# The last triangular system on GpSimd, the third with a shorter lag, and W_down's sums from the second head pair on

## The chip, the core and the metric

The kernel runs on one core of a Trainium2 chip. A core has five engines that each work off a queue of their own in order: TensorE (PE), VectorE (DVE), ScalarE (ACT), GpSimd (POOL), and SyncE (SP), which here only starts DMAs. The metric is the device time of one execution in microseconds; lower is better.

## The reference

One layer of a trunk with two parallel branches, over 1024 tokens of width 1024, in float32. Cut to what matters:

```python
h = rmsnorm(x, g_mix[i]);  z = h @ w_in[i]
q, k, v = ...                                   # 8 FoX heads of 64, q and k RMS-normed
log_f = jax.nn.log_sigmoid(zf[..., 3 * FOX_WIDTH:] + b_f[i])
y_fox = fox_attention(q, k, v, log_f)           # causal, bias c_i - c_j, c = cumsum(log_f)
yr = rwkv7_scan(rh, decay, kh, vh, -kk, kk * ah)    # 8 heads, state 64 x 64, step by step
merged = gate_fox * (y_fox @ w_o_fox[i]) + gate_rwkv * (y_rwkv @ w_o_rwkv[i])
x = x + merged @ w_out[i]
x = x + (gelu(u[..., :D_FF]) * u[..., D_FF:]) @ w_down[i]      # u: conv of rmsnorm(x) @ w_up
x = x + sigmoid(rmsnorm(x) @ w_ple_gate) * (p @ w_ple_up)
```

## The kernel before

The RWKV scan is done in chunks of 64 tokens. For each of four head pairs `rwkv_pre` projects r, k and v and builds, per chunk and head, a lower triangular system that is stored to HBM as `Ad`. `tsolve` inverts its two 32 x 32 diagonal blocks for all 16 chunks and both heads of a pair at once: it loads them as `tA` (four DMAs), copies the start into `tT` on GpSimd, and then makes 30 steps that depend on each other, each a product into `tt` and a sum into `tT`. Step j has ((j+1)//2) x (31-j) elements in each partition, 15 to 128, 2600 over all steps. The result goes to HBM as `Td`, and, turned by two ScalarE copies into `tX`, as `Ud`. The systems of head pairs 0 to 2 run beside `rwkv_pre` of the next pair, the last one beside attention's first projections.

Attention works in head pairs too. `fox_z` projects q, k and v (and, for pair 0, the forget inputs `ft`) in eight blocks of 128 tokens, called block 0 to 7 here. Each block takes one PSUM tile z of a pool of two. ScalarE copies it out (z, V, ft, sq) and VectorE takes V's rest and sums (ss); after blocks 3 and 7 sm, a square root (st) and a few small VectorE operations give the scale, and GpSimd scales four blocks of z at once (L759). `gate_early` makes 512 columns of a gate in one z tile, so its two halves take the tiles of blocks 6 and 7. `forget` turns ft into the forget row: ScalarE's abs, exp and ln (fe), L908 and L909 on VectorE, the prefix fpre, two products on PE (L917, L918), a copy fc, two transposes (L927) and a store (`cd`), which comes back as cb, spread over all partitions; VectorE adds it to the scores. `fox_qk` turns z into q and k, and is interleaved with `forget` and the gate. `fox_w` of the next pair splits weights in two parts (fwh, fwl), the second of three on GpSimd.

`down_sums` prepares W_down for a product scheme with fewer multiplications: for each of 11 pairs of blocks it loads two rows of blocks into `wt`, makes four subtractions on GpSimd and stores four sums as `wd`. It has one buffer.

Which work is emitted beside which is set by `interleave`, in which each part names its costs and a total, and the part that is least far along comes next:

```python
    live = [[g, n, 0.0] for g, n in parts]
    while live:
        it = min(live, key=lambda e: e[2] / e[1])
        try:
            it[2] += next(it[0]) or 0.0
```

A lag such as `yield self.tlag` is a cost without work. Emission isn't the last word: the framework that builds the program places instructions in each engine's queue by estimates of its own, so that the first six pairs of `down_sums` stand in GpSimd's queue under the RWKV part, where no code names them. The functions that the diff touches:

Of the kernel before, what the change touches and what calls it, by code (L numbers as in the profile page):

```python
# [20 lines left out]
P = 128  # L21
# [6 lines left out]
HP = 4  # L28
DFF = 2816
NFB = DFF // P  # L30
# [22 lines left out]
def flat(gens):  # L53
    for g in gens:
        yield from g
# [7 lines left out]
def interleave(*parts):  # L63
# [7 lines that stand above are left out]
        except StopIteration:  # L71
            live.remove(it)


def merge(*gens):

    live = list(gens)
    while live:
        for g in list(live):
            try:  # L80
                yield next(g)
            except StopIteration:
                live.remove(g)


class Net:
# [409 lines left out]
    def tsolve(self, hp):  # L496

        nc, tp = self.nc, self.tp
        tA = tp.tile([P, 32, 32], F32, name="tA", tag="tA", bufs=1)
        tT = tp.tile([P, 16, 32], F32, name="tT", tag="tT", bufs=1)
        tX = tp.tile([P, 32, 16], F32, name="tX", tag="tX", bufs=1)
        tmp = tp.tile([P, 144], F32, name="tt", tag="tt", bufs=1)
        Ad, Td, Ud = self.Ad[hp], self.Td[hp], self.Ud[hp]
        for q in range(2):
            for d in range(2):  # L510
                p0 = q * 64 + d * 32
                ds = slice(d * 32, d * 32 + 32)
                nc.sync.dma_start(tA[p0:p0 + 32], Ad[ds, :, ds].rearrange("s b t -> b s t"))
        yield self.tlag
        for q in range(2):
            r = slice(q * 64, q * 64 + 64)
            nc.gpsimd.tensor_copy(tT[r], tA[r, q:32:2, :])
        for j in range(1, 31):
            n, m = 31 - j, (j + 1) // 2
            tv = tmp[:, 0:m * n].rearrange("p (c i) -> p c i", i=n)  # L520
            nc.vector.tensor_mul(tv, tA[:, j:j + 1, j + 1:32].broadcast_to([P, m, n]),
                                 tT[:, 0:m, j:j + 1].broadcast_to([P, m, n]))
            nc.vector.tensor_add(tT[:, 0:m, j + 1:32], tT[:, 0:m, j + 1:32], tv)
            yield (2 * m * n / 960.0 + 0.13)
        for q in range(2):
            r = slice(q * 64, q * 64 + 64)
            nc.vector.memset(tT[r].rearrange("p a b -> p (a b)")[:, q:512:34], 1.0)
            for d in range(2):
                nc.sync.dma_start(Td[d, :, q:32:2, :], tT[q * 64 + d * 32:q * 64 + d * 32 + 32])
            r = slice(q * 64, q * 64 + 32)  # L530
            nc.scalar.copy(tX[r].rearrange("p b m -> p m b"), tT[r])
            nc.sync.dma_start(Ud[:, :, q * 16:q * 16 + 16], tX[r])
# [903 lines left out]
    def body(self, stop):  # L1436
        nc, a = self.nc, self.a
# [63 lines left out]
        self.cw = 160.0  # L1501
        self.lora_w()
        self.p1, close_p1 = self.pool("rw", side="right")
        self.tlag = 30.0
        for hp in range(HP):
            side = [(self.tsolve(hp - 1), 40.0)] if hp else []
            if hp == HP - 1:
# [9 lines left out]
        self.fp, close_fp = self.pool("fox", side="right")  # L1517
        self.kl = None
        zV, qk = [], []
        self.tlag = 12.0  # L1520
        self.wt, close_wt = self.pool("wt", side="left")
        self.wd2 = {n: self.tc.dram_tile([NFB // 2, P, 512], F32, name="wd" + n) for n in ("t1", "t2", "t3", "t4")}

# [3 lines left out]
        for hp in range(HP):  # L1527
            att = self.fox_att(hp, qk, zV[1])
            if hp + 1 < HP:
                zV, qk = [], []  # L1530
                interleave((att, 23.0), (self.fox_z(hp + 1, self.fox_w(hp + 1), zV), 31.5),
                           (self.down_sums(range(hp * 4, min(hp * 4 + 4, NFB // 2))), 12.0),
                           *([(flat([self.tmerge(2 * hp - 2, z_tile), self.tmerge(2 * hp - 1, z_tile)]), 24.0)] if hp else []))
                interleave((merge(self.last, flat([[0.0] * 3, self.fox_qk(zV[0], qk)])), 6.0), (self.gate_early(hp + 2), 10.4))
            else:
                n = HP + 1

                def rest():
                    yield from att
                    yield from self.last  # L1540
                interleave((rest(), 25.0), (flat([self.gate_early(j) for j in range(n, self.early)]),
                                            10.4 * (self.early - n)))
        close_ps()
        close_fp()
        close_fwp()
# [68 lines left out]
        m = []  # L1614
# [150 lines left out]
        for q in range(2):  # L1765
            for tb in range(4):
                if q == 0:
                    b = next(hi)
# [44 lines left out]
```

## Time and profile before

| | us |
|---|---|
| runs, median of 3 | 1881.25 (1880.01 to 1883.6) |
| profiled execution, its own time | 1872.82 |
| its span, first to last instruction | 1870.9 |
| PE busy | 1807.9 |
| VectorE busy | 1205.0 |
| ScalarE busy | 782.7 |
| GpSimd busy | 356.4 |

Of a row of a timeline the first number is the start, the second the duration, both in us; in brackets stands how long the engine was idle before it, and what it waited for. Durations and gaps belong to the profiled execution, the medians to separate runs without a profile. Names are those of the tiles, with L and a line number of the kernel before. After the change lines behind the first edit are two higher.

### The profile page before, as it was taken

What the parts mean: (1) busy time and instruction counts of PE and PEld (TensorE: products, weight loads), DVE (VectorE), ACT (ScalarE), POOL (GpSimd) and SP (SyncE); (2) the same over time, 40 slices, a digit from 0 to 9 for tenths busy, and PEclk for the clock granted to TensorE, in tenths of its full rate; (3) what the DMA queues carried; (4) which work ended last, traced back from release to release, by engine and by line L of the source; (5) the groups of instructions that cost most, each with busy time, mean ns of one, the idle gap of its engine ahead of it and who ended that gap; (6) DMA issues with size and microseconds to landing.
All of it is one profiled execution on the core that took longest, in us unless ns stands there. A gap on an engine that the chain in (4) does not pass through costs nothing.

```text
span 1870.9 us, 28292 instructions
## 1 busy us (share of the span) xinstructions
PE 1807.9 (97%) x10867; PEld 1484.4 (79%) x10867; DVE 1205.0 (64%) x2382; ACT 782.7 (42%) x1236; POOL 356.4 (19%) x251
## 2 busy tenths in 40 slices
PE   6999998799999999999999999999999999999999
PEld 5877778688988776666778988888888888888898
DVE  7537754767565734544436188999899986566752
ACT  4543252567676631122362244434343344434431
POOL 4321001330000000000013303554444531000000
PEclk9999999899999999999999999999999999999999
DMA  6667447542221255444375123333223328755431
GB/s 199 204 190 200 130 108 197 151 157 81 46 75 48 60 142 150 131 137 132 95 258 169 62 91 85 113 109 101 91 96 116 102 96 315 238 194 178 145 114 46
DMA packets 295085, 250.29 MB, mean 134 GB/s; under 512 B 80200, under 2 KB 235550, under 8 KB 294951
## 3 DMA queue, kind: packets, MB, share of 16 engines
q1 hardware_dynamic: 230071, 220.40, 37.4%
q10 hardware_dynamic: 64880, 28.09, 5.9%
q8 instruction: 86, 1.41, 0.3%
q14 instruction: 48, 0.39, 0.1%
HBM read 171.07 MB, written 77.37 MB: 133 GB/s over the span
## 4 chain that ended last, share of the span: by engine, by line
PE 65%; DVE 2%; DMA 2%; ACT 1%; issue 1%; SPq 0%; POOL 0%; ACTq 0%; DVEq 0%; POOLq 0%
PE pu L1155 8%; PE pu L1156 8%; PE pu L1157 8%; PE pu L1333 3%; PE pu L1332 3%; PE pu L1331 3%; PE zt L228 3%; PE zt L229 3%; PE zt L227 3%; PE zt L986 2%; PE zt L988 2%; PE zt L236 2%; PE zt L237 2%; PE zt L987 2%; PE zt L238 2%; PE yps L636 1%
## 5 line engine op out<-in xcount | busy, mean ns | idle before, releaser
L1331 PE MATMUL pu<-op 128*128 128x512 f32 x276 | 107.7, 390 | 0.0
L1333 PE MATMUL pu<-op 128*128 128x512 f32 x276 | 107.4, 389 | 0.0
L1332 PE MATMUL pu<-op 128*128 128x512 f32 x276 | 107.4, 389 | 0.0
L207 ACT CAST wh<-wr 128x1024 fp32r<-128x1024 f32 (+1 forms) x43 | 38.1, 890 | 123.2 <-PE zt L237 78.0
L236 PE MATMUL zt<-hah,wh 128*128 128x512 f32 (+1 forms) x200 | 80.6, 404 | 0.0
L237 PE MATMUL zt<-hal,wh 128*128 128x512 f32 (+1 forms) x200 | 78.8, 394 | 0.0
L236 PE MATMUL zt<-hbh,wh 128*128 128x512 f32 (+1 forms) x200 | 78.8, 394 | 0.0
L237 PE MATMUL zt<-hbl,wh 128*128 128x512 f32 (+1 forms) x200 | 78.3, 391 | 0.0
L238 PE MATMUL zt<-hbh,wl 128*128 128x512 f32 (+1 forms) x200 | 78.1, 390 | 0.0
L238 PE MATMUL zt<-hah,wl 128*128 128x512 f32 (+1 forms) x200 | 77.7, 389 | 0.0
L1165 DVE SCALAR_TENSOR_TENSOR u<-c,par,u 128x1023 f32<-128x1023 f32 x44 | 73.5, 1672 | 3.4 <-ACT u L1164 3.4
L208 DVE TENSOR_TENSOR op<-vh,op 128x1024 fp32r<-128x1024 f32 x38 | 45.4, 1222 | 45.1 <-ACT op L207 31.7
L1164 ACT ACTIVATE u<-c,par 128x1024 f32<-128x1024 f32 x44 | 54.6, 1243 | 47.5 <-DVE c L1241 37.6
L1166 DVE SCALAR_TENSOR_TENSOR u<-c,par,u 128x1022 f32<-128x1022 f32 x44 | 73.5, 1672 | 0.7
L1155 PE MATMUL pu<-hah,wh 128*128 128x512 f32 x176 | 70.3, 400 | 0.0
L1155 PE MATMUL pu<-t,vr 128*128 128x512 f32 x176 | 69.5, 395 | 0.5 <-DVE t L1073 0.5
L1156 PE MATMUL pu<-hal,wh 128*128 128x512 f32 x176 | 69.8, 397 | 0.0
L1157 PE MATMUL pu<-hah,wl 128*128 128x512 f32 x176 | 69.8, 396 | 0.0
L1156 PE MATMUL pu<-t,vr 128*128 128x512 f32 x176 | 69.4, 394 | 0.0
L1157 PE MATMUL pu<-t,vr 128*128 128x512 f32 x176 | 69.4, 394 | 0.0
L1156 PE MATMUL pu<-vl,vh 128*128 128x512 f32 x176 | 69.2, 393 | 0.0
L1155 PE MATMUL pu<-vh 128*128 128x512 f32 x176 | 69.0, 392 | 0.0
(534 smaller groups left out, 5603.6 us busy)
## 6 DMA issues: line engine op xcount, KB each, us to landing
X<-Xd SPq DMA_DIRECT2D x28, 448.0 KB
wt<-in_w_down SPq DMA_DIRECT2D x22, 512.0 KB
wdt<-wt SPq DMA_DIRECT2D x44, 256.0 KB
wr<-in_w_up SPq DMA_DIRECT2D x22, 512.0 KB
rr<-in_w_up SPq DMA_DIRECT2D x22, 512.0 KB
wr<-in_w_in ACTq DMA_DIRECT2D x21, 512.0 KB
mda<-u SPq DMA_DIRECT2D x33, 256.0 KB
mds<-sm SPq DMA_DIRECT2D x33, 256.0 KB
```

Source lines behind the costliest of these rows:

```text
L227: nc.tensor.matmul(ps, lhsT=lh, rhs=rh, start=(i == 0), stop=False)
L236: nc.tensor.matmul(o, lhsT=H[:, k, :], rhs=hh[:, k, :], start=(k == 0), stop=False)
L237: nc.tensor.matmul(o, lhsT=H[:, k, :], rhs=hl[:, k, :], start=False, stop=False)
L238: nc.tensor.matmul(o, lhsT=L[:, k, :], rhs=hh[:, k, :], start=False, stop=(k == NKB - 1))
L1155: nc.tensor.matmul(ps, lhsT=wh[:, k, :], rhs=bh[:, k, :], start=k == 0, stop=False)
L1156: nc.tensor.matmul(ps, lhsT=wh[:, k, :], rhs=bl[:, k, :], start=False, stop=False)
L1157: nc.tensor.matmul(ps, lhsT=wl[:, k, :], rhs=bh[:, k, :], start=False, stop=k == 3)
L1165: nc.vector.scalar_tensor_tensor(u[:, 1:T], c[:, 0:T - 1], cw(1), u[:, 1:T], op0=ALU.mult, op1=ALU.add)
L1166: nc.vector.scalar_tensor_tensor(u[:, 2:T], c[:, 0:T - 2], cw(0), u[:, 2:T], op0=ALU.mult, op1=ALU.add)
L1331: nc.tensor.matmul(ps[tb], lhsT=AH[:, j, ts], rhs=BH[:, j], start=f, stop=False)
L1332: nc.tensor.matmul(ps[tb], lhsT=AH[:, j, ts], rhs=BL[:, j], start=False, stop=False)
L1333: nc.tensor.matmul(ps[tb], lhsT=AL[:, j, ts], rhs=BH[:, j], start=False, stop=l)
```

## The change

`tsolve` takes its engine from the head pair: the last one's 60 operations and two memsets go to GpSimd. The lag is a constant for each pair, and the third has 12 in place of 30. `down_sums` no longer starts with head pair 0: pairs of blocks 0 to 3 are emitted with head pair 1, 4 to 7 with head pair 2, and 8 to 10 with the last.

```diff
+        ve = nc.gpsimd if hp == HP - 1 else nc.vector
...
-        yield self.tlag
+        yield (30.0, 30.0, 12.0, 12.0)[hp]
         for q in range(2):
             r = slice(q * 64, q * 64 + 64)
             nc.gpsimd.tensor_copy(tT[r], tA[r, q:32:2, :])
         for j in range(1, 31):
...
-            nc.vector.tensor_mul(tv, tA[:, j:j + 1, j + 1:32].broadcast_to([P, m, n]),
+            ve.tensor_mul(tv, tA[:, j:j + 1, j + 1:32].broadcast_to([P, m, n]),
                                  tT[:, 0:m, j:j + 1].broadcast_to([P, m, n]))
-            nc.vector.tensor_add(tT[:, 0:m, j + 1:32], tT[:, 0:m, j + 1:32], tv)
+            ve.tensor_add(tT[:, 0:m, j + 1:32], tT[:, 0:m, j + 1:32], tv)
...
-            nc.vector.memset(tT[r].rearrange("p a b -> p (a b)")[:, q:512:34], 1.0)
+            ve.memset(tT[r].rearrange("p a b -> p (a b)")[:, q:512:34], 1.0)
...
-        self.tlag = 30.0
...
-        self.tlag = 12.0
...
-                           (self.down_sums(range(hp * 4, min(hp * 4 + 4, NFB // 2))), 12.0),
+                           *([(self.down_sums(range(hp * 4 - 4, hp * 4)), 12.0)] if hp else []),
...
-                                            10.4 * (self.early - n)))
+                                            10.4 * (self.early - n)), (self.down_sums(range(8, NFB // 2)), 12.0))
```

On GpSimd, at the end of the first projections, stood before the copies of the last system (tT_2585), W_down's pair seven (wt_4531), the next weights' fwl and z's two scalings:

```order
L759 TENSOR_TENSOR z_2572<-z_2572,ss_2568 128x1024
L517 COPY tT_2585<-tA_2584 64x512 x2
L1259 TENSOR_TENSOR wt_4531<-wt_4531 128x512
L208 TENSOR_TENSOR fwl_3073<-gwr_3078,fwh_3072 128x8x128
L1260 TENSOR_TENSOR wt_4531<-wt_4531 128x512
L1261 TENSOR_TENSOR wt_4531<-wt_4531 128x512
L1262 TENSOR_TENSOR wt_4531<-wt_4531 128x512
L759 TENSOR_TENSOR z_2572<-z_2572,ss_2568 128x1024
```

Now the copies come ahead of z's first scaling, the 60 operations follow it, with the four subtractions of pair seven among the later ones, and this is how they end; fwl and z's second scaling come only then:

```order
L529 MEMSET tT_2585 64x16
L523 TENSOR_TENSOR tt_2587<-tA_2584,tT_2585 128x15
L525 TENSOR_TENSOR tT_2585<-tT_2585,tt_2587 128x15
L1261 TENSOR_TENSOR wt_5846<-wt_5846 128x512
L208 TENSOR_TENSOR fwl_3073<-gwr_3078,fwh_3072 128x8x128
L761 TENSOR_TENSOR z_2572<-z_2572,ss_2568 128x1024
L1262 TENSOR_TENSOR wt_5846<-wt_5846 128x512
```

On ScalarE, at the end of pair 0's projections, z_2816 is the tile of block 6 and z_2864 that of block 7. The copies tX of the last system stood some 30 rows further down, in the next pair's projections:

```order
L750 ACTIVATE sq_2857<-z_2816 128x256
L743 COPY z_2572<-z_2864 128x256
L745 CAST V_2573<-z_2864 128x2x64
L207 CAST fwh_3072<-fwr_3074 128x8x128
L748 COPY ft_2574<-z_2864 128x8
L750 ACTIVATE sq_2915<-z_2864 128x256
L207 CAST fwh_3072<-gwr_3078 128x8x128
```

Now they stand between block 6 and block 7:

```order
L752 ACTIVATE sq_2857<-z_2816 128x256
L533 COPY tX_2586<-tT_2585 32x16x32 x2
L745 COPY z_2572<-z_2864 128x256
L747 CAST V_2573<-z_2864 128x2x64
L207 CAST fwh_3072<-fwr_3074 128x8x128
L750 COPY ft_2574<-z_2864 128x8
L752 ACTIVATE sq_2915<-z_2864 128x256
L207 CAST fwh_3072<-gwr_3078 128x8x128
```

On TensorE, behind the gate's second half (z_2959), the first block of the next pair's projection (z_3104) began in one piece before:

```order
L238 MATMUL z_2959<-hbh_66,gwl_2929 128x512
L733 MATMUL z_3104<-fwh_3072,hah_64 128x384 x8
L733 MATMUL z_3104<-fwh_3072,hal_65 128x384
L927 MATMUL sc_3039<-ident_77,fc_3021 8x128 x4
L733 MATMUL z_3104<-fwh_3072,hal_65 128x384 x7
L733 MATMUL z_3104<-fwl_3073,hah_64 128x384 x2
L927 MATMUL sc_3045<-ident_77,fc_3021 8x128 x4
L733 MATMUL z_3104<-fwl_3073,hah_64 128x384 x4
L789 MATMUL sc_3059<-ident_77,z_2572 128x128 x4
L733 MATMUL z_3104<-fwl_3073,hah_64 128x384 x2
L738 MATMUL z_3223<-fwh_3072,hah_64 128x384
```

Now the transposes of z's second half and the second forget product (L920) stand at its start, and the forget row's transposes come earlier in it:

```order
L238 MATMUL z_2959<-hbh_66,gwl_2929 128x512
L783 MATMUL sc_3024<-ident_77,z_2572 128x128 x4
L735 MATMUL z_3104<-fwh_3072,hah_64 128x384
L920 MATMUL z_3018<-fpre_2972,ones_85 128x64
L735 MATMUL z_3104<-fwh_3072,hah_64 128x384 x5
L929 MATMUL sc_3039<-ident_77,fc_3021 8x128 x4
L735 MATMUL z_3104<-fwh_3072,hah_64 128x384 x2
L735 MATMUL z_3104<-fwh_3072,hal_65 128x384 x6
L929 MATMUL sc_3045<-ident_77,fc_3021 8x128 x4
L735 MATMUL z_3104<-fwh_3072,hal_65 128x384 x2
L791 MATMUL sc_3059<-ident_77,z_2572 128x128 x4
L735 MATMUL z_3104<-fwl_3073,hah_64 128x384 x8
```

The first forget product moved two rows of three products down, and the second from between the gate's products into the projection. Further on attention's transposes stand among fewer projection products than before.

## Rows read from the trace of the kernel before

**Rows 1.** The page, busy time and share of the span by engine.

```profile
PE 1807.9 (97%) x10867; PEld 1484.4 (79%) x10867; DVE 1205.0 (64%) x2382; ACT 782.7 (42%) x1236; POOL 356.4 (19%) x251
```

**Rows 2.** Windows: length, busy us by engine, clock, DMA share, GB/s.

```profile
316.00:317.00 1.00, 1.00 (x8) 1.00 (x7) 0.20 (x1) 0.54 (x2) 0.00 (x0) 1.00 0.00 0
...
340.00:350.00 10.00, 4.34 (x19) 3.08 (x18) 9.76 (x26) 3.63 (x7) 5.47 (x4) 0.75 0.62 186
350.00:360.00 10.00, 8.95 (x38) 7.12 (x37) 9.74 (x20) 7.43 (x12) 6.19 (x4) 0.74 0.57 209
```

**Rows 3.** Timeline of PE, 338 to 370 us.

```profile
338.80 0.40 PE L236 MATMUL z<-hbh,gwh 128*128 128x512 f32 x1
...
348.30 0.69 PE L917 MATMUL z<-ft,triu 128*128 128x64 f32 x2 [5.66 <-DVE ft L909]
348.74 0.77 PE L236 MATMUL z<-hbh,gwh 128*128 128x512 f32 x1
...
362.54 0.34 PE L738 MATMUL z<-fwh,hah 128*128 128x384 f32 x1
...
369.78 0.45 PE L738 MATMUL z<-fwh,hah 128*128 128x384 f32 x1 [2.58 <-ACT sq L750]
```

**Rows 4.** Timeline of DVE, 280 to 381 us.

```profile
280.59 1.22 DVE L208 TENSOR_TENSOR fwl<-fwr,fwh 128x1024 fp32r<-128x1024 f32 x1
...
336.34 2.38 DVE L755 TENSOR_SCALAR sm<-ss 128x16 f32<-128x16 f32 x1
...
348.02 0.22 DVE L909 TENSOR_TENSOR ft<-ft,fe 128x64 f32<-128x64 f32 x1
...
380.71 0.28 DVE L818 CUSTOM_DVE_ANT_0 pr<-sc,cb 128x128 f32<-128x128 f32 x1
```

**Rows 5.** Timeline of ACT, 333 to 368 us.

```profile
333.40 0.37 ACT L743 COPY z<-z 128x256 f32<-128x256 f32 x1 [2.94 <-PE z L740]
...
333.83 1.06 ACT L207 CAST fwh<-fwr 128x1024 fp32r<-128x1024 f32 x1
...
338.76 0.21 ACT L244 ACTIVATE st<-sm 128x16 f32<-128x16 f32 x1 [2.54 <-DVE sm L755]
...
342.48 0.26 ACT L907 ACTIVATE fe<-fe 128x64 f32<-128x64 f32 x1
...
365.76 2.15 ACT L531 COPY tX<-tT 32x512 f32<-32x512 f32 x2 [1.44 <-DVE tT L523]
```

**Rows 6.** Groups of POOL by shape: busy us, mean ns of one, idle before.

```profile
L1262 POOL TENSOR_TENSOR wt<-wt 128x512 f32<-128x512 f32 x11 | 14.1, 1284 | 0.9
...
L208 POOL TENSOR_TENSOR fwl<-gwr,fwh 128x1024 fp32r<-128x1024 f32 x4 | 9.6, 2392 | 79.9 <-ACT fwh L207 41.8 <-PE ps L451 24.1 <-PE tr L843 13.9
L517 POOL COPY tT<-tA 64x512 f32<-64x512 f32 x8 | 4.9, 609 | 104.6 <-ACT rt L244 54.5 <-DVE rn L249 31.3 <-DMA tA<-Ad 18.7
...
L208 POOL TENSOR_TENSOR fwl<-rf,fwh 128x64 fp32r<-128x64 f32 x1 | 0.9, 942 | 3.7 <-ACT fwh L207 3.7
...
L1805 POOL MEMSET const-bfloat16-1.0<- 128x1 bf16 x1 | 0.1, 111 | 0.0
```

**Rows 7.** Timeline of POOL, 42 to 339 us.

```profile
42.24 1.30 POOL L1261 TENSOR_TENSOR wt<-wt 128x512 f32<-128x512 f32 x1
43.61 1.29 POOL L1262 TENSOR_TENSOR wt<-wt 128x512 f32<-128x512 f32 x1
...
281.06 0.94 POOL L208 TENSOR_TENSOR fwl<-rf,fwh 128x64 fp32r<-128x64 f32 x1 [3.71 <-ACT fwh L207]
...
319.79 1.90 POOL L759 TENSOR_TENSOR z<-z,ss 128x1024 f32<-128x1024 f32 x1 [21.72 <-DMA wt<-in_w_down]
...
336.29 2.40 POOL L208 TENSOR_TENSOR fwl<-gwr,fwh 128x1024 fp32r<-128x1024 f32 x1 [12.01 <-ACT fwh L207]
```

**Rows 8.** Timeline of SP's issues at 370 us.

```profile
370.42 1.13 SPq L881 DMA_DIRECT2D cb<-cd  x2
```

**Rows 9.** The tile tt: count, durations in ns (min/median/max), starts, forms.

```profile
L521 DVE TENSOR_TENSOR tt<-tA,tT x120: 167/258/1870, 146.0 to 365.3; 128x110 f32<-128x110 f32 x12, 128x120 f32<-128x120 f32 x12, 128x30 f32<-128x30 f32 x8, 128x56 f32<-128x56 f32 x8
```

## The prediction

> **What bounds the kernel now.** The first view is the busy time of each engine: TensorE (PE) has 97% of the span, the next engine 64% [rows 1]. So time is won or lost only where PE stands still or runs at the lower clock, and I read one stretch of the trace for that: the change from the RWKV part to attention, from 320 to 380 us. The view by stretches shows PE busy for 4.34 of 10 us from 340 to 350 and 8.95 of 10 from 350 to 360, at a granted clock of 0.75 and 0.74 [rows 2]. PE's timeline says why. The second half of the gate's product begins at 338.80. At 348.30 PE has stood for 5.66 us, since the forget bias (L917) needs ft from VectorE's line L909. Behind that stall the products run at the lower of the two clocks, 1.2 GHz in place of 2.4: one that takes 0.40 us at 338.80 takes 0.77 at 348.74. The second block of attention's next projection begins at 362.54, that is 23.7 us after the gate's second half, and PE stands once more for 2.58 us before 369.78 [rows 3].
>
> VectorE's timeline says why L909 is late (348.02). Its operand fe was ready when ScalarE's L907 ended at 342.74 [rows 5]; in between VectorE worked off operations of the last triangular system that stand ahead of it in its queue. It was also held up by GpSimd: sm, 16 elements wide, took 2.38 us from 336.34, while GpSimd's fwl ran from 336.29 to 338.69 [rows 4, 7]. The 2.58 us are the system's too: ScalarE's copies of its result, tX, ran from 365.76 to 367.91 after a wait for VectorE's L523 [rows 5], and sq, which releases PE's z tile, stood behind them.
>
> **The change, part by part.** In what follows T is the end of the last triangular system on GpSimd.
>
> *The lag of the third system, 30 to 12.* VectorE's queue is the same up to the last system. On SP the six stores of the third system's result now stand ahead of five stores of Xd3. SP waits for that result a little, so the loads of tA for the last system come some 2 us later (an estimate: five issues at the 0.57 of [rows 8], less a wait that overlaps). No DMA moved anything from 316 to 317 [rows 2], so tA had landed by then; now by about 318. GpSimd copies it in two pieces of 0.61 [rows 6], done before z's first scaling starts at 319.79 [rows 7]. Cost: nothing, with some 0.5 us of cover; behind that it would move T one for one.
>
> *W_down's sums from the second pair on.* 22 loads, 44 stores and 44 subtractions stay. Pairs one to six stand in GpSimd's queue as before, under RWKV. Pair seven now stands inside the last system, pair eight behind it. Their price is in T.
>
> *The last system on GpSimd.* 60 dependent operations leave VectorE, and with them the 5.66 and 2.58 us. What they cost on GpSimd the trace does not show, so I bound it. Two-input operations take 1.284 us at 512 elements and 2.392 at 1024 [rows 6], which gives 0.176 fixed and 2.16 ns an element; from one dependent operation to the next there are 1.37 us for 1.30 of work [rows 7], so 0.08 more. The 30 steps have 2600 elements each for product and sum. 60 x 0.256 + 5200 x 2.16 ns = 26.6 us. Below: a one-element memset (0.111) as the fixed part and the copy's rate (0.609 for 512) give 14.5 us. Above: the only small two-input row, 64 elements, took 0.942 [rows 6]; 60 x 1.02 = 61 us. I take 26.6. That row began at 281.06, while VectorE's own subtraction (280.59 for 1.22) was on, and ended 0.19 after it [rows 4, 7], so most of it was waiting.
>
> The system starts behind z's first scaling, which ends at 321.69 [rows 7]: 321.8. Four subtractions of pair seven stand inside it, 4 x 1.37 = 5.5. T = 321.8 + 26.6 + 5.5 = 353.9.
>
> The Trainium skill (GPSIMD Engine Reference, section 4.1, Engine selection) speaks against the move: elementwise work belongs on VectorE, and GpSimd is about twice as slow with two inputs. The long rows agree (2.392 on GpSimd, 1.22 on VectorE for 1024). For the short ones no row tells; by that rule T would be 363, which is a rival below.
>
> *Who waits for T.* In ScalarE's new queue tX stands right behind sq of block 6, ahead of everything that empties block 7. Before, z's copy of block 7 began at 333.40 [rows 5]. PE's second gate half reuses block 7's z tile, so it can't begin at 338.80. From T on: two copies 2.2, z and V 0.55, the fwh cast 1.06, ft and sq 0.5, and PE starts again at T + 4.3 = 358.2, which is 19.4 us late.
>
> *What is late next.* A second cast lets GpSimd begin fwl at T + 5.2, to T + 7.6. VectorE's sm meets it as at 336.34 and ends near T + 8.0. ScalarE's run from st to the end of fe took 4.0 us (338.76 to 342.74 [rows 5]); with one q (0.7) now inside it ends at T + 12.7, and the forget bias comes at T + 13.0. PE gets there about then, since it starts at the lower clock, as at 348.74. ScalarE goes on: k twice, q, a cast, k twice, q, gz, in all 5.7 us of about 0.7 each, to T + 18.4, and only gz frees the tile for the next projection (L735, first row). Then a cast, fc, the two transposes of the forget row, which also wait for VectorE's gwl and q. The projection's first block ends at T + 23.9 = 377.8, that is 19.6 us after PE's start. Before, it was 23.7 us for the same work, ending at 362.5. The shift is **+15.3 us**.
>
> *Behind it.* The 2.58 us are gone, since tX is no longer there. Attention starts earlier in PE's order and with less projection between its links. Its bias row cb stands on SP behind the store of gz, pair eight's second load and two stores, and I have it in place near T + 30.5 (from issue to use no row tells; at most 10 us, from the issue at 370.42 to the first use at 380.71 [rows 4, 8]). I put 2 us on that. Some 340 rows of PE's queue later its order is the same again, and at 97% busy PE has little slack to give anything back.
>
> **Sum.** +15.3 - 2.6 + 2 = +14.7 us. On the profiled execution's 1872.8 (span 1870.9 and 1.9 around it) that is 1887.5. The median of the runs lies 8.4 above the profiled one; I carry it over: **1896**.
>
> **Rivals.**
> - *GpSimd at twice VectorE's time.* VectorE's median is 0.258 [rows 9]; 60 x (0.516 + 0.08) = 35.8, T = 363, +24, 1905. For it: the long rows. Against: the fixed parts need not double. This is what the rule of the Trainium skill above would do.
> - *GpSimd at 0.94 an operation.* T = 389, +49, 1931. For it: the only small row. Against: VectorE was on at the time.
> - *cb comes later.* SP is in order; 6 us more, with VectorE's first attention operation in front of all that empties z: 1902. For it: the gz store ahead of it waits until T + 18.
> - *GpSimd at the lower bound.* T = 341.8, +2.6, 1884: not to be told from no change.
> - *The other side: ScalarE isn't held.* If the system ended by 333.4, PE would start its second half at 338.80, lose the 5.66 and 2.58 us and part of the lower clock: 7 to 13 us faster, 1868 to 1874. It decides at T = 339.2, where the sum is zero: 60 operations in 11.9 us, 0.20 each. For it: VectorE is full in this stretch, and the stalls that go are real. Against: a memset of one element takes 0.11, and 0.08 lies between dependents.
>
> **How the numbers follow.** Chances: forecast 0.60, twice VectorE's time 0.13, cb 0.09, 0.94 an operation 0.05, lower bound 0.07, the other side 0.06. The forecast's own range, with 0.1 us an operation either way (6 us) and 2 for what I put on cb, is 1888 to 1904. Leaving out the dear case, the cheap one and the other side (0.18), the range is 1885 to 1912. 0.2% is 3.8 us, about what a measurement of this kernel can tell from no change: faster 0.06, same 0.07, slower 0.87.
>
> **What would show it.** Right: on GpSimd 60 short operations of 0.2 to 0.5 us that end near 354; ScalarE idle from block 6's sq until then, waiting for GpSimd; PE idle from 338.8 to about 358 and then at the lower clock; a first projection block that ends near 378; no wait of 2.58 us behind it. Wrong: tX with no wait, or T before 340; a PE that passes 338.80 without a stop; a shift that is gone by the end of attention's first head pair.

## The result, and the profile after

The changed kernel takes 1886.57 us (median of 9 runs, 1884.91 to 1891.87), the kernel before in the same comparison 1877.05 us (9 runs, 1872.23 to 1883.6). The ratio is 1.0054, with a 95% interval of 1.0038 to 1.0071: slower, by some 10 us. The profiled execution has a span of 1883.9 us and takes 1885.6, that is 13.0 and 12.8 more than before. The page's busy line answers to [rows 1]: GpSimd has 19 us more, VectorE 20 less, and PE the same:

```profile
PE 1806.8 (96%) x10867; PEld 1485.1 (79%) x10867; DVE 1185.4 (63%) x2320; ACT 783.4 (42%) x1237; POOL 375.4 (20%) x313
```

The windows answer to [rows 2]. From 340 to 350 us no engine but GpSimd is busy, and from 350 to 360 PE is busy for 3.16 us at a granted clock of 0.50, which is the lower of the two levels, 1.2 GHz. From 370 to 380 the mean is 0.83:

```profile
340.00:350.00 10.00, 0.00 (x0) 0.00 (x0) 0.00 (x0) 0.00 (x0) 8.83 (x21) 0.72 0.40 131
350.00:360.00 10.00, 3.16 (x10) 2.58 (x11) 3.77 (x4) 4.97 (x8) 5.46 (x11) 0.50 0.42 65
360.00:370.00 10.00, 6.84 (x30) 4.84 (x28) 6.12 (x20) 9.28 (x15) 2.08 (x2) 0.92 0.41 102
370.00:380.00 10.00, 9.11 (x49) 8.48 (x50) 4.29 (x7) 6.33 (x12) 3.47 (x3) 0.83 0.88 257
```

GpSimd's timeline of the changed kernel: the system's first and last operations, one of pair seven's subtractions of W_down in between, and what stands behind.

```profile
322.35 0.24 POOL L523 TENSOR_TENSOR tt<-tA,tT 128x30 f32<-128x30 f32 x1
...
334.27 0.42 POOL L523 TENSOR_TENSOR tt<-tA,tT 128x128 f32<-128x128 f32 x1
334.64 1.29 POOL L1261 TENSOR_TENSOR wt<-wt 128x512 f32<-128x512 f32 x1
335.90 0.46 POOL L525 TENSOR_TENSOR tT<-tT,tt 128x128 f32<-128x128 f32 x1
...
352.42 0.23 POOL L525 TENSOR_TENSOR tT<-tT,tt 128x15 f32<-128x15 f32 x1
...
357.80 2.38 POOL L208 TENSOR_TENSOR fwl<-gwr,fwh 128x1024 fp32r<-128x1024 f32 x1 [3.93 <-ACT fwh L207]
361.78 1.91 POOL L761 TENSOR_TENSOR z<-z,ss 128x1024 f32<-128x1024 f32 x1 [1.61 <-DVE ss L249]
```

So T, the end of the system, is 352.65. ScalarE's timeline has waited for it since 331.16, with all of block 7 behind:

```profile
352.68 2.12 ACT L533 COPY tX<-tT 32x512 f32<-32x512 f32 x2 [21.52 <-POOL tT L525]
354.82 0.37 ACT L745 COPY z<-z 128x256 f32<-128x256 f32 x1
...
356.40 0.39 ACT L752 ACTIVATE sq<-z 128x256 f32<-128x256 f32 x1
...
360.43 0.37 ACTq L216 DMA_DIRECT2D gwr<-in_w_in  x1
...
364.95 0.26 ACT L909 ACTIVATE fe<-fe 128x64 f32<-128x64 f32 x1
```

PE's timeline answers to [rows 3]: the gate's second half at 356.84 in place of 338.80, the forget bias, and the end of the projection's first block (the row of L740) at 378.31 in place of 362.54. Of the wait of 5.66 us 1.66 are left, and that of 2.58 is gone.

```profile
356.84 0.80 PE L236 MATMUL z<-hbh,gwh 128*128 128x512 f32 x1 [17.18 <-ACT sq L752]
365.52 0.43 PE L919 MATMUL z<-ft,triu 128*128 128x64 f32 x2 [1.66 <-DVE ft L911]
370.89 0.45 PE L735 MATMUL z<-fwh,hah 128*128 128x384 f32 x1 [2.01 <-ACT gz L975]
378.31 0.34 PE L740 MATMUL z<-fwh,hah 128*128 128x384 f32 x1
```

One more number is needed to compare runs. Executions differ by some microseconds in parts that no edit touches. I therefore take the **stretch** from the start of attention's first projection on PE to the start of the last two stores of Wd on SP. These are its ends, two rows of the kernel before and then two of the changed one:

```profile
297.30 2.98 PE L733 MATMUL z<-fwh,hah 128*128 128x392 f32 x8 [1.28 <-ACT bt L486]
589.40 2.08 SPq L567 DMA_DIRECT2D Wd<-tT  x2
```

```profile
296.68 2.98 PE L735 MATMUL z<-fwh,hah 128*128 128x392 f32 x8 [1.28 <-ACT bt L486]
603.82 1.80 SPq L569 DMA_DIRECT2D Wd<-tT  x2
```

| kernel | start | last Wd | stretch | ratio of times to before, 95% |
|---|---|---|---|---|
| before, first and second trace | 297.30, 297.15 | 589.40, 590.87 | 292.1, 293.7 | 1, 1.0008 (0.9995 to 1.0021) |
| changed, first and second trace | 296.68, 296.56 | 603.82, 601.75 | 307.1, 305.2 | 1.0054, 1.0058 (1.0043 to 1.0072) |
| e1 tX on GpSimd | 301.81 | 610.09 | 308.3 | 1.0084 (1.0067 to 1.0100) |
| e2 system alone | 296.46 | 592.73 | 296.3 | 1.0005 (0.9991 to 1.0018) |
| e3 the rest alone | 298.29 | 595.45 | 297.2 | 1.0008 (0.9997 to 1.0020) |
| e4 half of the system | 297.26 | 597.46 | 300.2 | 1.0029 (1.0016 to 1.0043) |
| e5 e1 and fwl | 296.85 | 598.28 | 301.4 | 1.0029 (1.0014 to 1.0045) |
| e6 e5 and z's scaling | 296.63 | 599.88 | 303.3 | 1.0037 (1.0019 to 1.0055) |
| e7 e2 and tX | 297.22 | 584.65 | 287.4 | 0.9957 (0.9940 to 0.9975) |
| e9 e6 and cb | 296.38 | 601.23 | 304.9 | 1.0052 (1.0036 to 1.0069) |
| e10 e7 and fwl | 296.08 | 582.38 | 286.3 | 0.9958 (0.9943 to 0.9972) |
| e11 before and tX | 294.10 | 585.51 | 291.4 | 0.9983 (0.9970 to 0.9995) |

The stretch grew by 13.3 us (mean of two traces each), the time by 10.

### The profile page after: what moved, and what is told of

Read it like the earlier page. It is cut to its first block, busy times and chain, and to the rows that moved or that the text cites. A ratio compares the mean times of both kernels' runs of the same rounds, so it can differ in the third digit from the quotient of the medians.

```text
span 1883.9 us, 28277 instructions
## 1 busy us (share of the span) xinstructions
PE 1806.8 (96%) x10867; PEld 1485.1 (79%) x10867; DVE 1185.4 (63%) x2320; ACT 783.4 (42%) x1237; POOL 375.4 (20%) x313
## 4 chain that ended last, share of the span: by engine, by line
PE 64%; DVE 2%; DMA 2%; ACT 1%; issue 1%; SPq 0%; POOL 0%; ACTq 0%; POOLq 0%; DVEq 0%
PE pu L1157 8%; PE pu L1158 8%; PE pu L1159 8%; PE pu L1333 3%; PE pu L1335 3%; PE pu L1334 3%; PE zt L228 3%; PE zt L227 3%; PE zt L229 3%; PE zt L988 2%; PE zt L236 2%; PE zt L990 2%; PE zt L237 2%; PE zt L989 2%; PE zt L238 2%; PE yps L638 1%
```

## The experiments

Theory A: the loss is ScalarE's wait at tX, and goes when tX is taken out of its queue. Theory B: the system on GpSimd is late for everything that stands behind it, on GpSimd itself and in other queues, and tX is only the first place.

**e1, tX alone.** Only this moves; every other queue is that of the changed kernel.

```diff
-            nc.scalar.copy(tX[r]...
+            (nc.gpsimd.tensor_copy if hp == HP - 1 else nc.scalar.copy)(tX[r]...
```

> The changed kernel with one difference in all queues: the two copies tX of the last system are made by GpSimd, right behind the system, and no longer by ScalarE between z's blocks 6 and 7. Theory A (the whole loss is ScalarE's wait at tX): PE begins the gate's second half near 339.5 in place of 356.84 us, the 17.2 us stall is gone, and the kernel is as fast as before or up to 8 us faster. Theory B (the system on GpSimd is late for all that stands behind it, and ScalarE's queue only shows the first place): the second half of the gate begins near 339.5, but ScalarE then stands at the issue of the load of gwr, whose buffer GpSimd's fwl frees, and fwl still stands behind the system: it ends near 357.6 in place of 360.18. fe, and with it the forget bias of PE, then comes only 2 to 4 us earlier than in the changed kernel (365.5), PE waits there for 10 to 15 us, and the kernel is 2 to 4 us faster than the changed one, so still some 6 to 8 us slower than before.

Theory A fell. PE's waits from 320 to 450 us, with the total, the count and the longest in us:

```profile
PE z L919 <- DVE ft L911: 20.4, 1, 20.4
```

and ScalarE's timeline, with the place where it now stands, the load of gwr, behind GpSimd's fwl (362.62 to 364.96 here):

```profile
364.99 0.37 ACTq L216 DMA_DIRECT2D gwr<-in_w_in  x1
365.46 0.59 ACT L975 COPY gz<-z 128x512 f32<-128x512 f32 x1 [22.11 <-DMA tA<-Ud]
```

The releaser that the second row names is a load that the copy has no use for; the issue ahead of it in the queue needs fwl, and it started 0.03 us behind fwl's end. L919 came 68.3 us after the start of the stretch, against 68.8 in the changed kernel: theory B's 2 to 4 us were not won either. The start of the stretch is 5 us late, some 3 of them because PE waited 3.41 us near 116 us for VectorE, which waited for a transfer of the RWKV part (0.32 in the changed kernel); by time e1 is the slowest of all, and how much of its 1.0084 is that, is open.

**e2 and e3, one part alone.** e2 is the kernel before with `ve = nc.gpsimd if hp == HP - 1 else nc.vector` and its uses; e3 is the changed kernel with `ve = nc.vector`.

> The kernel before with the last system on GpSimd alone; the lags and the sums of W_down as before. By its order fwl and z's second scaling stand amid the system on GpSimd, and ScalarE comes to tX only behind the first k. The system then ends near 357 us (352.7 and 4.3 for those two). Theory A, in the form that a wait at the start of block 7 is what costs: no such wait, so as fast as before or faster by up to 10 us. Theory B: PE passes 339 without a stop and VectorE's L909 is no longer late, but ScalarE is held at tX until 357, and fc, which PE's transposes of the forget row need, stands behind it: PE waits near 350 to 361, and the kernel is 3 to 8 us slower than before.

> The changed kernel with the last system back on VectorE: the lag of the third system and the place of W_down's sums as changed, and nothing else. Theory A and B alike: no long wait of ScalarE for GpSimd, so the 17 us stall is gone and the time is that of the kernel before within 4 us either way. Rival (the loss comes from the moved sums of W_down or from the lag): slower than before by more than 5 us, as the changed kernel.

Neither part costs what both cost together: 1.0005 and 1.0008. In e2 PE stood still from 352.6 to 361.9, as expected behind tX on ScalarE (there is q behind it, and then fc); the wait for the forget bias was not expected. PE's waits:

```profile
PE sc L782 <- DVE q L785: 9.4, 1, 9.4
PE z L918 <- DVE ft L910: 4.2, 1, 4.2
```

The stretch grew by 3.4 us over the mean of before, the time by nothing that shows, so the expected loss of 3 to 8 us is missed (the interval ends at 3.4 us). The system ended at 358.14 there, 5.5 us later than in the changed kernel. Only the lag and W_down tell e2 from the changed kernel, and what they change is the order in the queues: in e2 fwl and z's scaling stand amid the system (at 339.77 and 347.74) and not behind it, and tX stands behind the first k. e3 moves a wait of 10.0 us to L919, since ScalarE comes to tX ahead of fe; its time is that of before, its stretch 4.3 us longer.

**e4, half of the system.**

```diff
+            v = nc.vector if j < 16 else ve
-            ve.tensor_mul(tv, ...
+            v.tensor_mul(tv, ...
-            ve.tensor_add(tT...
+            v.tensor_add(tT...
```

> The changed kernel with the first 15 of the 30 steps of the last system on VectorE and the other 15 on GpSimd. The four subtractions of W_down's pair seven then stand ahead of GpSimd's part, while VectorE works. VectorE's part should end near 333.5, GpSimd's 30 operations take 12.4 us (336.4 to 352.7 in the changed kernel less three subtractions), so the system ends near 346, 6.6 us earlier. Theory A or B (the end of the system sets PE's restart): PE begins the gate's second half some 6.6 us earlier (near 350), and the kernel is some 5 to 7 us faster than the changed one, 2 to 4 us slower than before. Rival (the price is in contention between GpSimd and VectorE, or in PE's clock, not in when the system ends): time within 2 us of the changed kernel.

GpSimd's part began at 336.42, where I had taken 333.5, and ended at 349.39, 3.3 us earlier than in the changed kernel and not 6.6. GpSimd's last row and PE's restart:

```profile
349.16 0.23 POOL L526 TENSOR_TENSOR tT<-tT,tt 128x15 f32<-128x15 f32 x1
353.31 0.79 PE L236 MATMUL z<-hbh,gwh 128*128 128x512 f32 x1 [6.48 <-ACT sq L753]
```

The restart comes 3.9 us after T, against 4.2 in the changed kernel: the end of the system sets it. The time falls by 0.25%, 4.7 us, a little less than the 5 to 7 expected.

**e5, e6 and e9, the other things behind the system taken away one by one.** Each holds the edits of the one before, and e5 those of e1. In e5 the fwl of head pair 1 is made by VectorE, in e6 z's second scaling too, in e9 ScalarE issues cd and the first pair's cb.

```diff
-            self.split(raw, ..., nc.gpsimd if j == 1 else None)
+            self.split(raw, ..., nc.gpsimd if j == 1 and hp != 1 else None)
...
-                nc.gpsimd.tensor_mul(z4, z4, s4)
+                (nc.vector if hp == 0 and tb == 7 else nc.gpsimd).tensor_mul(z4, z4, s4)
...
-            self.nc.sync.dma_start(cb, self.cd...
+            (self.nc.scalar if hp == 0 else self.nc.sync).dma_start(cb, self.cd...
-        nc.sync.dma_start(self.cd, crow)
+        nc.scalar.dma_start(self.cd, crow)
```

> The changed kernel with tX copied by GpSimd, as in the run before with that name, and the one fwl subtraction of GpSimd that stands behind the system (head pair 1's k weights) moved to VectorE; every queue is otherwise the same. ScalarE then waits neither at tX nor at the load of gwr. Theory B (each thing that stands behind the system on GpSimd holds PE in turn): the forget bias is in time or nearly, and PE now stops at the transposes of z's second half, whose scaling on GpSimd stands behind the system, the copies and one W_down subtraction: some 62.8 us after the start of attention's first projection, in place of 71.6 (changed kernel) and 72.3 (tX moved alone). The stretch from that projection's start to the last store of Wd, 292.1 us before and 307.1 in the changed kernel, is then near 298, and the kernel some 9 us faster than the changed one. Theory C (with tX moved alone the time was lost somewhere else, in PE's clock or in transfers): the stretch stays above 304.

As theory B had it, PE stopped at z, 64.6 us after the start (62.8 expected). But the forget bias was not in time: PE waited 4.79 us for it, since ScalarE stood at the load of gwr after all, until a store of W_down's sums had landed (e6 below tells why). PE's timeline, then ScalarE's:

```profile
349.62 0.69 PE L919 MATMUL z<-ft,triu 128*128 128x64 f32 x2 [4.79 <-DVE ft L911]
361.45 1.12 PE L783 MATMUL sc<-ident,z 128*128 128x128 f32 x4 [7.62 <-POOL z L761]
```

```profile
344.54 0.38 ACTq L216 DMA_DIRECT2D gwr<-in_w_in  x1
345.01 0.59 ACT L975 COPY gz<-z 128x512 f32<-128x512 f32 x1 [6.55 <-DMA wdt<-wt]
```

The gain over the changed kernel is 0.25 to 0.29%, 5 us, where 9 were expected. Part of the rest is the system, which began 0.6 us later and ended 3.4 us later, at 356.01. Some of its operations on GpSimd grow longer beside two fwl subtractions on VectorE, of which one was moved there and the other is no longer held up by ScalarE; e6 shows it best, in which GpSimd's rows met VectorE's fwl of 336.15 (1.37 us) and of 337.98 (1.43 us):

```profile
336.40 1.44 POOL L525 TENSOR_TENSOR tT<-tT,tt 128x128 f32<-128x128 f32 x1
337.92 0.41 POOL L523 TENSOR_TENSOR tt<-tA,tT 128x120 f32<-128x120 f32 x1
338.41 1.29 POOL L525 TENSOR_TENSOR tT<-tT,tt 128x120 f32<-128x120 f32 x1
```

> As the run with tX and fwl moved, and z's second scaling on VectorE too: nothing that PE or ScalarE needs in this stretch stands behind the system on GpSimd any more. Theory B: none of the long waits is left, neither those of the changed kernel (17.2) nor those of before (5.66 and 2.58), and the stretch takes 282 to 286 us in place of 292.1 before and 307.1 changed; the kernel is 5 to 10 us faster than before. Rival: VectorE, which now has the system taken off and two operations of 1.2 to 1.5 us put on, is late for the forget bias or for attention, or the result of the system is late for its merge: the time of before or worse.

The wait for z went, and no gain on e5 shows: 303.3 us, and a time of 1.0037. That is the time that the rival had named, but not its reason: VectorE stood idle for 8.31 us, waiting for cb, before attention's first scores. PE's waits, then the rows of VectorE, ScalarE and SP that lie behind them:

```profile
PE sc L815 <- DVE st L820: 7.6, 1, 7.6
PE z L919 <- DVE ft L911: 5.9, 1, 5.9
PE sc L791 <- ACT cb L930: 3.3, 1, 3.3
```

```profile
381.47 0.29 DVE L820 CUSTOM_DVE_ANT_0 pr<-sc,cb 128x128 f32<-128x128 f32 x1 [8.31 <-DMA cb<-cd]
```

```profile
345.61 0.37 ACTq L216 DMA_DIRECT2D gwr<-in_w_in  x1
346.08 0.59 ACT L975 COPY gz<-z 128x512 f32<-128x512 f32 x1 [7.62 <-DMA wdt<-wt]
...
363.38 0.41 ACTq L706 DMA_DIRECT2D fwr<-in_w_in  x1
363.83 0.57 ACT L930 COPY cb<-sc 8x512 f32<-8x512 f32 x1 [5.11 <-DMA Ud<-tX]
```

```profile
360.54 0.57 SPq L534 DMA_DIRECT2D Ud<-tX  x1
...
365.39 8.18 SPq L1267 DMA_DIRECT2D wdt<-wt  x2
373.67 0.30 SPq L932 DMA_DIRECT2D cd<-cb  x1
```

ScalarE waits at two loads for stores with which they share no data. The program says why: a DMA counts up one of eight completion semaphores, which SP and ScalarE use in turn, and an issue waits until the one before it on its semaphore has landed. So stand the two in ScalarE's queue of e6, with what they wait for (DMAHW0 to DMAHW7 are the eight semaphores):

```
L216 DMA gwr_3818<-in_w_in 128x8x128 [waits DMAHW0_49,DVE_49]
L706 DMA fwr_3973<-in_w_in 128x8x128 [waits DMAHW3_49,Activation_49]
```

The store ahead on semaphore 0 is one of W_down's pair seven, whose subtractions stand amid the system; the one on semaphore 3 is the store of Ud, behind tX. And on SP the bias row cd stands behind pair eight's first two stores, which took until 373.6. So the system reaches ScalarE and VectorE through the DMAs as well.

> As the run with tX, fwl and z's scaling moved, and for the first head pair the store of the bias row (cd) and its two loads (cb) are issued by ScalarE and not by SP, where they stood behind the stores of the system's result and behind W_down's pair eight. That run had PE waits of 7.6 us for attention's first scores (VectorE at 381.47 behind cb), 5.9 for the forget bias and 3.3 for the copy of the bias row. Theory B, with SP as one more queue behind the system: the 7.6 us go, the other two stay, and the stretch from attention's first projection to the last store of Wd falls from 303.3 to 293 to 297 us; the kernel is as fast as before within 0.25%. Rival (attention is late for another reason): the stretch stays above 300.

cb came 3.8 us earlier (VectorE's first scores at 377.66 in place of 381.47), but the stretch did not fall (304.9), and the time was 1.0052 where that of before was expected. ScalarE now holds the issue itself, behind the landing of cd, and a store on SP comes late:

```profile
372.58 0.37 ACTq L883 DMA_DIRECT2D cb<-cd  x1
373.00 0.38 ACT L752 ACTIVATE sq<-z 128x256 f32<-128x256 f32 x1 [4.05 <-DMA cd<-cb]
...
396.18 0.37 ACT L869 COPY yf<-pv 64x256 f32<-64x256 f32 x1 [7.56 <-DMA yFd<-yf]
```

PE's wait for cb fell from 7.6 to 2.6 us, and 2.6 and 6.3 us came up behind these two rows. Theory B is borne out in kind at each step. As a sum it is not: each hold that is taken away uncovers the next, and a price for one, read from a trace in which others cover it, says little.

**e7, e10 and e11, from the kernel before.** e11 moves only tX, e7 the system and tX, e10 also the fwl that stands amid the system. Lags and W_down are as before.

> The kernel before with the last system on GpSimd and its tX copies there too; lags and W_down's sums as before. fwl and z's second scaling stand amid the system by its order. The run with the system alone had one wait of 9.38 us, for q that stands behind tX on ScalarE. Theory B: that wait goes, the 4.22 us for the forget bias stays, and the stretch from attention's first projection to the last store of Wd takes 285 to 288 us in place of 296.3 (system alone) and 292.1 (before); the kernel is 4 to 7 us faster than before. Theory C: PE waits for something else that is late, and the stretch stays above 292.

> The kernel before with the two tX copies of the last system on GpSimd and nothing else. The 2.58 us wait of PE behind ScalarE's tX goes, the 5.66 us stay. The stretch (292.1 and 293.7 us in two traces) is then 289 to 291 us and the kernel 2 to 3 us faster than before. If the move of the system itself brings nothing, this run is as fast as the one with the system and tX on GpSimd (0.9957); if it is the move that pays, it is 3 to 5 us slower than that one.

> As the run with the system and tX on GpSimd (287.4 us for the stretch), and the fwl subtraction that stood amid the system moved to VectorE. If the 4.2 us that PE still waits for the forget bias come from ScalarE's wait for that fwl at the load of gwr, they shrink to under 1 us, and the stretch takes 282 to 285 us. If ScalarE is held there by something else that the system delays (a store of W_down's sums), the wait and the stretch stay as they are, within 1 us.

e7 is the fastest with e10: 1868.5 us where before took 1876.58, a ratio of 0.9957, or 8 us where 4 to 7 were expected. GpSimd's timeline of e7:

```profile
340.37 2.39 POOL L208 TENSOR_TENSOR fwl<-gwr,fwh 128x1024 fp32r<-128x1024 f32 x1
...
348.35 1.90 POOL L760 TENSOR_TENSOR z<-z,ss 128x1024 f32<-128x1024 f32 x1
...
360.36 0.23 POOL L524 TENSOR_TENSOR tT<-tT,tt 128x15 f32<-128x15 f32 x1
```

The system ends at 360.59, 7.9 us later than in the changed kernel, and the stretch is 20 us shorter. e11 gives 0.9983, a gain of 3 us; the rest to 0.9957, some 5 us, is the system's move (the two intervals overlap a little, and the stretches differ by 4.0). PE has still 4.2 us for the forget bias in e7; in e10 they are gone, and a wait of 4.6 us for the transposes of z takes their place, whose scaling on GpSimd ran from 348.21 to 350.11: the time is the same, and the stretch of 282 to 285 us that was expected is missed.

**e8 and e12, the two kernels again.**

> The kernel before, unchanged, for a second trace of it: how far the stretch from attention's first projection to the last store of Wd (292.1 us) and the start of that projection (297.3) move from one execution to the next. Both theories: the stretch within 2 us, the start within 5 us; the time within 0.1% of before.

> The changed kernel once more, for a second trace: the stretch (307.1 us) and PE's 17.2 us wait within 2 us, the time within 0.15% of what was measured (1.0054 of before).

Both stretches lie within 2 us of the first, 293.7 and 305.2, and PE's wait is the same to 0.02 us (17.18 and 17.20). The spans moved more, 1870.9 to 1875.6 and 1883.9 to 1879.3, so a difference of two single executions can be off by 5 us or more.

## Why the prediction was right

- **T.** Start 322.35 for 321.8, end 352.65 for 353.9. The median operation took 0.360 (product) and 0.381 us (sum), 0.08 between dependent ones. By the spacing of the starts the four subtractions added some 1.1 each, 4.5 for 5.5, which leaves 25.8 for the system where 26.6 was predicted. The line through GpSimd's long operations held for the short ones; the row of 0.942 us was mostly waiting, for 65 elements took 0.32 here. By the Trainium skill (GPSIMD Engine Reference, section 4.1) a two-input operation on GpSimd takes about twice VectorE's time. The short products here took 1.4 times VectorE's median of 0.258 [rows 9].
- **ScalarE held at tX, PE's restart at T + 4.3.** Right: 21.52 us of wait, restart at T + 4.2. e4 shows that it is T that sets it. PE came back at 1.2 GHz, with 0.80 us for a product, as predicted.
- **What is late next.** fwl's end T + 7.6 (7.5), fe T + 12.7 (12.6), L919 T + 13.0 (12.9), gz T + 18.4 (18.2): right to 0.2 us. The VectorE operation that fwl held up was L905, not sm. The first block ended at T + 25.7 and not 23.9. gz had freed its tile when predicted; what was too small is the block itself, 7.4 us for 5.5. PE had stood still for 2.01 us just ahead of it, and from 372 to 375 us the granted clock was 0.50 once more. At half the clock 3 us hold the work of 1.5, so that accounts for some 1.5 us, an estimate, of the 1.9 that the block took too long. The prediction had the lower clock at the restart and not a second time. Since T was 1.3 early, the shift came to 15.8 for 15.3, so two misses nearly cancelled.
- **Behind it.** The 2.58 us went. cb was in use at T + 33.2 for 30.5, and attention stood 2.8 us for ph. At the last store of Wd the first pair of traces is 14.4 us apart (predicted 14.7), the second 10.9; the stretch grew by 13.3 on average.
- **The number.** 1896 was predicted and 1886.6 measured. That is below the forecast's own 1888 to 1904 and 1.6 us above the low end of the whole range, so the time alone says little for the forecast; T and the waits do. The step that was off is the carry-over: I added the 8.4 us by which the median of three runs lay above the profiled execution, and with more runs that median is 1875.9 to 1877.05, 4 to 5 us lower. The rest, another 4 to 5 us, is the shift: 9.5 to 11 us by the medians for 14.7. Where it went isn't shown: at the last store of Wd 13.3 us are still there, and from there to the end the changed kernel's two traces are 4.3 us shorter on average (1278.8 for 1283.1), where two traces of one kernel differ by 2.5 and 3.2.
- **The rival at the lower bound.** Its 14.5 us count the 2600 elements once and not for product and sum. With 5200, and 0.08 us between operations, its terms give 17.6, T near 345 and 1887. By the time alone this rival would have won; T = 352.65 rules it out.
- **The lag at no cost, W_down only in T.** By itself the pair of edits costs nothing that shows in the time (e3). Beside the system they cost nearly all: e7, which has the system and tX as e1 has them, differs from e1 in these edits alone, and takes 287.4 us where e1 takes 308.3. They are what put the system ahead of fwl and z's scaling, and cd behind pair eight's first two stores, ahead of which it stands in e7. The prediction read that from the queues but booked it under T. Which of the two edits does it, and what share each of these queues has, no run tells.
- **The other side.** It was priced at 7 to 13 us for a system that ends by 333.4. e7, in which tX is on GpSimd too, got 8 us with a system that ends at 360.59: T was not the only way to it.

## What to carry to other kernels

Before a slow chain is moved to an idle engine, list what stands behind its end in every queue: on that engine, at the copies of its result, and at the DMAs that store it. If that list holds anything the busiest engine needs soon, put it ahead of the chain's end or elsewhere. Here this weighed more than when the chain ended: e7's system ended 8 us later, in a kernel 18 us faster. With the list left as it was, the end did count (3.3 us earlier gave 4.7 in e4). Waits in series hide each other, so taking away one shows the next; a run of the whole version tells what a move is worth.

## What the runs showed of the hardware

- The row below is VectorE's L905 in the changed kernel, 64 elements wide. It took 2.26 us, while GpSimd's fwl ran from 357.80 to 360.18, and ended 0.08 us behind it; in e6, where GpSimd was between two short operations, it took 0.21. It goes the other way too: GpSimd's 1.44 and 1.29 us in e6, for operations that took 0.46 and 0.42 in the changed kernel.

```profile
358.00 2.26 DVE L905 TENSOR_TENSOR ft<-ft,bf 128x64 f32<-128x64 f32 x1
```

  The Trainium skill (SBUF — State Buffer, Terms) says that the two engines share a pair of ports, which one of them holds for a whole instruction. The rows agree: the shorter operation ended when the longer one was over.
- The issue of a load waited 5 to 8 us for stores without any data in common, by way of a shared completion semaphore (e5, e6, e9).
- GpSimd made the two tX copies in 2.12 us in e1, as fast as ScalarE in the changed kernel (2.12) and before (2.15 [rows 5]). In e6, where VectorE's gwl ran beside them from 357.92 for 1.23 us, they took 2.95.
